# A two-layer mixer encoder on one core: how the first quarter's modulation is summed, and in which order the start is issued

## The chip, the core and the metric

The kernel runs on one core of one Trainium2 chip. The metric is the time of one execution in device microseconds (us), lower is better; three runs of the kernel before gave 649.83, 650.28 and 650.92, median 650.28.

## The reference, cut to what matters

`x` is (1, 512, 1024), `c` is (1, 1024), and there are two layers. Cut to the parts around the change:

```
cs = jax.nn.silu(c)
for l in range(DEPTH):
    mod = cs @ w_ada[l] + b_ada[l]
    shift, scale, gate = jnp.split(mod, 3, axis=-1)
    h = rms_norm(x, norm_g[l]) * (1.0 + scale[:, None]) + shift[:, None]
    proj = h @ w_in[l]                       # 1024 x 3712
    ...                                      # A attention, B windowed attention, C retention
    oc = retention_bidir(qc, kc, vc.reshape(B, S, H_C, DV_C), ret_decay[l], gn_c[l])
    ...
    y = jnp.concatenate([oa, ob, oc], axis=-1) @ w_out[l]
    x = x + gate[:, None] * y
```

`retention_bidir` begins with `log_g = log_sigmoid(ret_decay)`, 8 numbers a layer.

## The kernel before, in words

The 512 tokens are four tiles t of 128, the 1024 features four **quarters** q of 256 (numbered 0 to 3; the first is also called quarter 1 in the change's title). A product of float32 accuracy is made of three float32r products: each operand is split into a part `hi`, rounded by ScalarE (ACT), and a rest `lo` that VectorE (DVE) subtracts.

The start of layer 0 runs quarter by quarter, and a quarter needs the following.

- **Modulation.** `class Start` sums `w_ada` over the 1024 numbers of `cs`, which lie as 8 rows r of 128 partitions. `load` brings two rows into a `raw` buffer (there are five), `row` adds one row to `ada_acc` (the first row of a quarter by ACT, the others by DVE, one 128x512 instruction each), and `close` sums `ada_acc` over the partitions with four matmuls of one moving column (`over_rows`, into `ada_ps`). DVE then makes `mod` of it, the shift and scale. `open` puts the bias in `ada_ps` first. In quarter 0 the rows in `PE_ROWS` go to TensorE (PE) instead.
- **x, turned.** `norm_x` makes `xn` (ACT sums squares, GpSimd takes the root, ACT and DVE scale), `turn_x` transposes four 128x128 blocks on PE into one PSUM tile `xps`, and ACT copies them to `xT`.
- **h.** `turn` makes `hT` (ACT, from `xT` and `mod`), the same unrounded as `h` (DVE), and `hL = h - hT` (DVE).
- **The weights.** `Wide` loads 768 columns of `w_in` as `whi` and `wlo` (three buffers each) and splits them: `stq` and `stB` are the rounded parts (ACT), `stk` and `stC` the rests (DVE).
- **The products.** One group is one (q, t): six products of 512 columns into `acc` and six of 256 into `scw`, at lines 338 (hi by hi), 339 (lo by hi) and 340 (hi by lo). Sixteen groups make the first chunk; `issue(lo, hi)` emits them.

The names in profile rows follow: `stq`/`stk` are the weights of quarters 0 and 2, `stB`/`stC` those of 1 and 3, and `whi`/`wlo` as operands of PE belong to the chunk that comes after (a plan of groups with loads and splits tied to group numbers, the same before and after).

The order of the first steps is the string `START`: each letter is a step (`x` loads and normalizes a token tile, `a` loads and adds two rows of quarter 0, `r` of quarter 1, `t` turns two token tiles of one quarter, `h` makes `h` for two token tiles, `w`/`v` load and `s` splits weights, `f` closes quarter 0). After it comes a loop over quarters 1 to 3, in which `close`, the next loads, `split`, `turn` and `issue` follow each other. A scheduler then sets each engine's own order; all engines work their lists in order, and all DMAs are issued by SyncE (SP). `setup` makes small tables, the last of them the decays: a chain of some 25 instructions of 16 elements on DVE.

Of the kernel before, what the change touches and what calls it, by code (L numbers as in the profile page):

```python
# [19 lines left out]
P = 128  # L20
# [33 lines left out]
PE_ROWS = (0, 2, 4, 5, 6, 7), (), (), ()  # L54


START = "xxbiaaataxfxwrthsttthttrvrrt"
# [18 lines left out]
_SMALL = {"lambda_q1": 32, "lambda_k1": 32, "lambda_q2": 32, "lambda_k2": 32, "ret_decay": 8,  # L76
# [12 lines left out]
N_PARAM = _params()  # L89
N_ONCE = _PARAM["qn_a"][0]  # L90
# [43 lines left out]
def encoder(ctx, tc, x, c, norm_g, w_ada, b_ada, w_in, w_out, params, consts, out):  # L134
# [91 lines left out]
    def setup_loads():  # L226
        once.append(ep.tile([P, N_ONCE], F32, name="once", tag="e"))
        dma(once[0], params[:, :N_ONCE])
        dma(prm, params[:, N_ONCE:])
        dma(cst[:, P:], consts[:, P:N_KEEP])  # L230

    def setup():
# [22 lines left out]


        NL = L * 8
        dec = pr("ret_decay").rearrange("p l n -> p (l n)")
# [231 lines left out]
    class Start:  # L490
# [11 lines left out]
        def open(self):  # L502
            q = self.q
            self.ps = ps = pv_p.tile([P, 2, 2], F32, name="ada_ps", tag="pv")
            self.a = self.line = None

            T.matmul(ps, bias[:2 * KD, 0], ident[:2 * KD].rearrange("p (a j k) -> p a j k", j=2, k=KD)[:, 0, :, 2 * q:2 * q + 2], start=True, stop=False)
# [18 lines left out]
        def close(self):  # L526
            q, ps = self.q, self.ps
            if self.a is not None:
                self.over_rows(self.a, ones[:, 0:1], self.line is None)
            if self.line is not None:  # L530
                z = one.tile([P, 512], F32, name="lsb", tag="s9")
                act(z[0:1], self.line[0:1])
                self.over_rows(z[0:1], ones[0:1, 0:1], True)
            m = self.m = one.tile([P, 2, 2], F32, name=f"mod0{q}")
            stt(m[:, 1], ps[:, 1], 1.0, ngt[:, 2 * q:2 * q + 2], OP.add, OP.mult)
            V.tensor_copy(m[:, 0], ps[:, 0])

        def turn(self, ts):
# [4 lines left out]
            for k in range(2):  # L543
# [4 lines left out]
                V.tensor_scalar(h[:, :n], x_, scale, shift, OP.mult, OP.add)  # L548
# [658 lines left out]
    def turn_x(t, q):  # L1207
        ps = acc_p.tile([P, 2, 2, P], F32, name="xps", tag="acc")
# [17 lines left out]
    def start_end():  # L1226
# [15 lines left out]
    for q in range(1, 4):  # L1242
# [56 lines left out]
```

## Time and profile before

| | us |
|---|---|
| median of three runs | 650.28 (649.83 to 650.92) |
| the profiled execution | 653.0 |
| its span in the profile | 651.2 |
| PE busy | 625.5 (96%) |
| DVE busy | 496.8 (76%) |
| ACT busy | 340.2 (52%) |
| GpSimd busy | 164.4 (25%) |

The profile shows one execution. Times in its rows count from the start of the span, and the profiled execution took 1.8 us more than its span. PE's own busy share counts matmuls that overlap, so that 96% says that PE nearly always has something in hand, not that it runs at its peak.

### The profile page before, as it was taken

What the parts mean: (1) busy time and instruction counts of PE and PEld (TensorE: products, weight loads), DVE (VectorE), ACT (ScalarE), POOL (GpSimd) and SP (SyncE); (2) the same over time, 40 slices, a digit from 0 to 9 for tenths busy, and PEclk for the clock granted to TensorE, in tenths of its full rate; (3) what the DMA queues carried; (4) which work ended last, traced back from release to release, by engine and by line L of the source; (5) the groups of instructions that cost most, each with busy time, mean ns of one, the idle gap of its engine ahead of it and who ended that gap; (6) DMA issues with size and microseconds to landing.
All of it is one profiled execution on the core that took longest, in us unless ns stands there. A gap on an engine that the chain in (4) does not pass through costs nothing.

```text
span 651.2 us, 10473 instructions
## 1 busy us (share of the span) xinstructions
PE 625.5 (96%) x3487; PEld 514.2 (79%) x3487; DVE 496.8 (76%) x1212; ACT 340.2 (52%) x750; POOL 164.4 (25%) x183
## 2 busy tenths in 40 slices
PE   6999999999999996999999999999999999899997
PEld 1878888987888873677779998997788787677786
DVE  1889776789978986997869374778997996677543
ACT  4744362666746665564434244455756567656410
POOL 1105462514360510200411041632323340010000
PEclk9799999999999998999999999999999999999999
DMA  9987123426565557476643322235555453603211
GB/s 315 334 290 207 40 82 88 133 91 152 147 177 167 125 172 175 141 254 224 185 169 96 90 72 67 77 101 154 142 171 137 142 142 103 163 32 139 89 64 65
DMA packets 87133, 93.03 MB, mean 143 GB/s; under 512 B 7044, under 2 KB 68132, under 8 KB 87080
## 3 DMA queue, kind: packets, MB, share of 16 engines
q1 hardware_dynamic: 87080, 92.37, 47.8%
q8 instruction: 28, 0.46, 0.3%
q14 instruction: 25, 0.20, 0.1%
HBM read 72.42 MB, written 4.19 MB: 118 GB/s over the span
## 4 chain that ended last, share of the span: by engine, by line
PE 77%; DVE 11%; issue 5%; POOL 3%; DMA 2%; ACT 2%; SPq 0%; POOLq 0%; ACTq 0%; DVEq 0%
PE acc L338 15%; PE acc L340 15%; PE acc L339 15%; PE tr L555 8%; PE pv L701 5%; PE sc L724 2%; PE acc L334 2%; PE acc L335 1%; PE acc L336 1%; DVE ada_acc L158 1%; PE sc L785 1%; DVE wlo L307 1%; PE sc L786 1%; PE line L519 1%; PE co L954 1%
## 5 line engine op out<-in xcount | busy, mean ns | idle before, releaser
L338 PE MATMUL acc<-whi,hT 128*128 128x384 f32 (+1 forms) x424 | 155.1, 366 | 0.0
L339 PE MATMUL acc<-wlo,hT 128*128 128x384 f32 (+1 forms) x424 | 152.3, 359 | 0.0
L340 PE MATMUL acc<-whi,hL 128*128 128x384 f32 (+1 forms) x424 | 152.0, 358 | 0.0
L307 DVE TENSOR_TENSOR wlo<-raw,whi 128x384 fp32r<-128x384 f32 (+1 forms) x130 | 81.8, 658 | 27.0 <-ACT whi L155 26.7
L198 POOL TENSOR_TENSOR qkss<-qkss,nhalf 128x4 f32<-128x4 f32 (+1 forms) x40 | 52.6, 1316 | 128.3 <-DVE qkss L570 125.7
L338 PEld LDWEIGHTS acc<-whi,hT 128*128 128x128 f32 x424 | 79.9, 188 | 6.1
L340 PEld LDWEIGHTS acc<-whi,hL 128*128 128x128 f32 x424 | 79.8, 188 | 6.2
L339 PEld LDWEIGHTS acc<-wlo,hT 128*128 128x128 f32 x424 | 79.9, 188 | 5.5
L155 ACT ACTIVATE whi<-raw 128x768 fp32r<-128x768 f32 (+2 forms) x67 | 59.6, 890 | 36.8 <-PE acc L340 34.0
L158 DVE SCALAR_TENSOR_TENSOR ada_acc<-raw,cs,ada_acc 128x512 f32<-128x512 f32 x86 | 64.4, 750 | 7.1 <-DMA raw<-in_w_ada_dram 5.9
L155 ACT ACTIVATE e<-sc,mx 128x512 f32<-128x512 f32 x64 | 43.9, 688 | 35.8 <-DVE mx L726 17.2
L726 DVE TENSOR_REDUCE mx<-sc 128x1 f32<-128x512 f32 x64 | 43.5, 685 | 9.6 <-PE sc L724 9.1
L155 ACT ACTIVATE sb<-sb,mx 128x512 f32<-128x512 f32 x48 | 34.4, 717 | 20.5 <-DVE mx L790 20.2
L701 PE MATMUL pv<-pt,v 128*64 128x256 f32 x320 | 40.1, 394 | 0.6 <-DVE pt L691 0.5
L155 ACT ACTIVATE pt<-tr 128x512 f32<-128x512 f32 x40 | 23.8, 596 | 24.2 <-PE tr L555 24.1
L790 DVE CUSTOM_DVE_ANT_0 sb<-sc,cst 128x512 f32<-128x512 f32 x48 | 32.1, 684 | 5.4 <-PE sc L786 3.5
L555 PE MATMUL tr<-cst,sb 128*128 128x128 f32 x192 | 30.5, 282 | 5.3 <-DVE nat L158 2.2
L701 PEld LDWEIGHTS pv<-pt,v 128*64 128x64 f32 x320 | 21.7, 140 | 16.6 <-DVE pt L691 5.3
L555 PEld LDWEIGHTS tr<-cst,sb 128*128 128x128 f32 x192 | 22.1, 142 | 15.8 <-ACT pt L155 7.3
L691 DVE COPY pt<-tr 128x512 f32<-128x512 f32 x40 | 27.4, 684 | 8.4 <-PE tr L555 8.4
L622 POOL TENSOR_TENSOR qkn<-qkraw,qkss 128x256 f32<-128x256 f32 x40 | 30.4, 760 | 5.8 <-DVE qkraw L618 2.0
L724 PE MATMUL sc<-stk,stq 96*128 96x512 f32 x64 | 27.3, 434 | 0.9 <-ACT e L155 0.9
(293 smaller groups left out, 1368.9 us busy)
## 6 DMA issues: line engine op xcount, KB each, us to landing
raw<-in_w_ada_dram SPq DMA_DIRECT2D x64, 256.0 KB, 4.8
raw<-in_w_in_dram SPq DMA_DIRECT2D x48, 192.0 KB, 2.6
raw<-in_w_in_dram SPq DMA_DIRECT2D x24, 384.0 KB, 3.9
raw<-in_w_in_dram SPq DMA_DIRECT2D x32, 256.0 KB, 3.6
raw<-in_w_ada_dram SPq DMA_DIRECT2D x16, 512.0 KB, 5.4
raw<-in_w_out_dram SPq DMA_DIRECT2D x32, 256.0 KB, 2.8
x<-in_x_dram SPq DMA_DIRECT2D x8, 512.0 KB, 3.5
stB<-nat SPq DMA_DIRECT2D x32, 128.0 KB, 2.3
```

Source lines behind the costliest of these rows:

```text
L155: A.activation(o, i, f, **kw)
L158: V.scalar_tensor_tensor(o, a, s, b, op0, op1)
L198: G.tensor_tensor(o, i, nhalf[:, :n], OP.pow)
L307: V.tensor_tensor(l2[:, z], r2[:, z], h2[:, z].bitcast(F32), OP.subtract)
L338: T.matmul(ps, ah, hi[i], start=s_, stop=False)
L339: T.matmul(ps, ah, lo[i], start=False, stop=False)
L340: T.matmul(ps, al, hi[i], start=False, stop=e_)
L555: T.transpose(ps[:, i, :], b, ident)
L701: T.matmul(self.pv[h * 64:h * 64 + 64, i * 256:i * 256 + 256], self.u.v[:, k, h * 64:h * 64 + 64], self.pt[h][:, k], start=k == 0, stop=k ...
L724: T.matmul(ps, self.u.stq[0:96, m, tok_(qt)], self.u.stk[0:96, m], start=True, stop=True)
L726: V.tensor_reduce(mx, ps, AX.X, OP.max, negate=True)
L790: V.tensor_tensor_reduce(sb, ps, cst[:, m0:m0 + S], 1.0, 3e38, OP.add, OP.min, mx)
```

## The change

Of quarter 0's rows, four instead of six go to PE, and each is used as a stationary operand with one moving column of `cs`, straight into `ada_ps`; the other four are added on ACT and DVE. The transposed blocks use the one PSUM buffer of tag `tr` instead of the four of tag `acc`. `START` is another order: `d` starts the decays' chain with a load of its own, the weights `w` and their split `s` come before the last two tiles of `x`, and `g` issues the groups of token tiles 0 and 1, then 2 and 3, of quarter 0 before the remaining transpositions. In quarters 2 and 3, and in half of quarter 1, `h` is made by ACT instead of DVE. In the loop each quarter's groups are issued in its own pass, and the small tables' loads (`setup_loads`) come before the next quarter's rows.

```
-PE_ROWS = (0, 2, 4, 5, 6, 7), (), (), ()
-START = "xxbiaaataxfxwrthsttthttrvrrt"
+PE_ROWS = (0, 2, 4, 6), (), (), ()
+START = "xxbidaaatawsfhgxxrthgttrttrvrtt"
...
+    def decays():
         NL = L * 8
-        dec = pr("ret_decay").rearrange("p l n -> p (l n)")
+        dec = one.tile([P, NL], F32, name="dec")
+        dma(dec, params[:, :N_DEC])
...
             if r in PE_ROWS[self.q]:
-                if self.line is None:
-                    self.line = acc_p.tile([P, 512], F32, name="line", tag="acc")
-                T.matmul(self.line[0:1], v, w, start=r == PE_ROWS[self.q][0], stop=r == PE_ROWS[self.q][-1])
+                self.over_rows(w, v)
...
             else:
-                stt(self.a, w, v, self.a, OP.mult, OP.add)
+                i = V.scalar_tensor_tensor(self.a, w, v, self.a, OP.mult, OP.add)
+                if self.q > 1 and r == 2:
+                    tc.keep_in_program_order(i)
...
-            if self.line is not None:
-                z = one.tile([P, 512], F32, name="lsb", tag="s9")
-                act(z[0:1], self.line[0:1])
-                self.over_rows(z[0:1], ones[0:1, 0:1], True)
...
-                V.tensor_scalar(h[:, :n], x_, scale, shift, OP.mult, OP.add)
+                if q > 1 or q and k:
+                    act(h[:, :n], x_, AF.Identity, bias=shift, scale=scale)
+                else:
+                    V.tensor_scalar(h[:, :n], x_, scale, shift, OP.mult, OP.add)
...
-        ps = acc_p.tile([P, 2, 2, P], F32, name="xps", tag="acc")
+        ps = tr_p.tile([P, 2, 2, P], F32, name="xps", tag="tr")
...
+        if q == 2:
+            setup_loads()
         if q < 3:
             mod = Start(q + 1)
             mod.load()
             first[q + 1].load()
-        if q == 2:
-            setup_loads()
         first[q].split()
         cur.turn(range(NT))
-        issue(4 * q - 4, 4 * q)
-    issue(12, 16)
+        issue(4 * q, 4 * q + 4)
```

Three places show how the engines' own orders move. Numbers behind a name tell buffers apart: `mod00` to `mod03` belong to quarters 0 to 3.

**DVE, around the end of quarter 0's sum.** Before (`ada_acc_164` is that sum, `xn` the normalized x, `ngt` the transposed norm gains):

```order
L1229 COPY ngt_113<-gps_198 128x8
L1205 TENSOR_SCALAR xn_146<-x1_94,rstd_147 128x512
L1205 TENSOR_SCALAR xn_136<-x0_93,rstd_137 128x512
L158 SCALAR_TENSOR_TENSOR ada_acc_164<-raw_166,cs_101,ada_acc_164 128x512
L570 TENSOR_SCALAR rstd_191<-rstd_191 128x1
L1205 TENSOR_SCALAR xn_189<-x2_95,rstd_191 128x512
L158 SCALAR_TENSOR_TENSOR mod00_211<-ada_ps_157,ngt_113 128x2
L536 COPY mod00_211<-ada_ps_157 128x2
```

Now (`ada_acc_198` is the sum, `lu`, `lz` and `lg` belong to the decays; twenty-three more of their instructions stand ahead of this piece, with two more additions among them):

```order
L274 TENSOR_SCALAR lu_159<-lu_159 128x16
L525 SCALAR_TENSOR_TENSOR ada_acc_198<-raw_223,cs_101,ada_acc_198 128x512
L275 TENSOR_TENSOR lu_159<-lu_159,lz_160 128x16
L159 SCALAR_TENSOR_TENSOR lg_117<-lu_159,lg_117 128x16
L159 SCALAR_TENSOR_TENSOR mod00_248<-ada_ps_189,ngt_113 128x2
L535 COPY mod00_248<-ada_ps_189 128x2
L550 TENSOR_SCALAR h_252<-xT0_126,mod00_248 128x256
L550 TENSOR_SCALAR h_256<-xT1_127,mod00_248 128x256
L385 TENSOR_TENSOR stk_236<-whi_231,stq_235 128x2x384
L551 TENSOR_TENSOR hL_119<-h_252,hT_118 128x256
L385 TENSOR_TENSOR stk_236<-wlo_232,stq_235 128x2x384
L551 TENSOR_TENSOR hL_119<-h_256,hT_118 128x256
```

The decays' chain and two more additions now stand ahead of `mod00`, and the splits of the weights directly behind it; x's third tile comes after them.

**PE, where quarter 2's sum over partitions stands.** Before (`ada_ps_415` is quarter 2's; the products around it are quarter 1's last group):

```order
L338 MATMUL acc_402<-stB_349,hT_118 128x512
L512 MATMUL ada_ps_415<-ones_104,ada_acc_417 128x1 x4
L339 MATMUL acc_402<-stC_350,hT_118 128x512
L340 MATMUL acc_402<-stB_349,hL_119 128x512
L338 MATMUL acc_402<-stB_349,hT_118 128x512
L339 MATMUL acc_402<-stC_350,hT_118 128x512
L340 MATMUL acc_402<-stB_349,hL_119 128x512
L338 MATMUL scw_124<-stB_349,hT_118 128x256
```

Now (`ada_ps_503` is quarter 2's, `ada_ps_611` quarter 3's):

```order
L341 MATMUL scw_124<-stB_438,hT_118 128x256
L342 MATMUL scw_124<-stC_439,hT_118 128x256
L343 MATMUL scw_124<-stB_438,hL_119 128x256
L515 MATMUL ada_ps_503<-ones_104,ada_acc_505 128x1 x4
L510 MATMUL ada_ps_611<-cst_103,bias_112 128x4
L341 MATMUL acc_259<-stq_541,hT_118 128x512
L342 MATMUL acc_259<-stk_542,hT_118 128x512
```

Before, eleven products of quarter 1 follow quarter 2's sum; now it stands behind quarter 1's last product and directly ahead of quarter 2's first. Quarter 3's sum moved in the same way, behind quarter 2's last product.

**ACT, between quarters 2 and 3.** Before (`ada_acc_520` is quarter 3's sum, its first row is ACT's):

```order
L155 ACTIVATE stq_453<-wlo_346 128x2x384
L155 ACTIVATE ada_acc_520<-raw_433,cs_101 128x512
L155 ACTIVATE hT_118<-xT4_130,mod02_430 128x512
L155 ACTIVATE hT_118<-xT5_131,mod02_430 128x512
L155 ACTIVATE stB_536<-whi_445 128x2x384
```

Now (`ada_acc_613` is quarter 3's):

```order
L156 ACTIVATE stq_541<-wlo_435 128x2x384
L156 ACTIVATE lsum_661<-lsum_661 128x4
L156 ACTIVATE hT_118<-xT4_130,mod02_518 128x512
L156 ACTIVATE h_548<-xT4_130,mod02_518 128x512
L156 ACTIVATE hT_118<-xT5_131,mod02_518 128x512
L156 ACTIVATE h_552<-xT5_131,mod02_518 128x512
L156 ACTIVATE ada_acc_613<-raw_525,cs_101 128x512
```

Quarter 3's first row stood ahead of the instructions that wait for `mod02`, and now stands behind four of them.

## Rows read from the trace of the kernel before

**Rows 1.** The page: the span, and the busy time of each engine.

```profile
span 651.2 us, 10473 instructions
PE 625.5 (96%) x3487; PEld 514.2 (79%) x3487; DVE 496.8 (76%) x1212; ACT 340.2 (52%) x750; POOL 164.4 (25%) x183
```

**Rows 2.** Busy time of each engine in stretches: stretch, its length, busy us (instructions) of PE, PE's weight loads, DVE, ACT and POOL, then the granted TensorE clock, the DMA engines' busy share and GB/s.

```profile
58.00:102.00 44.00, 44.00 (x256) 38.21 (x255) 35.80 (x122) 20.62 (x50) 21.99 (x20) 1.00 0.27 78
102.00:104.00 2.00, 0.85 (x7) 0.56 (x7) 1.30 (x5) 0.47 (x1) 0.00 (x0) 1.00 0.14 25
```

**Rows 3.** PE's instructions in order of time: the first main product of quarters 0, 1, 2 and 3, and of the next chunk (start us, duration us, engine, line, operation).

```profile
24.91 0.63 PE L338 MATMUL acc<-stq,hT 128*128 128x512 f32 x1
...
34.91 0.50 PE L338 MATMUL acc<-stB,hT 128*128 128x512 f32 x1
...
44.71 0.51 PE L338 MATMUL acc<-stq,hT 128*128 128x512 f32 x1
...
55.99 0.39 PE L338 MATMUL acc<-stB,hT 128*128 128x512 f32 x1
...
64.39 0.39 PE L338 MATMUL acc<-whi,hT 128*128 128x512 f32 x1
```

**Rows 4.** The chain that ended last, in order of time: start us, length us, engine, tile, line.

```profile
25.53 0.43 PE acc L339
...
26.55 0.24 PE acc L339
...
46.60 0.75 DVE ada_acc L158
...
48.18 0.70 DVE hL L549
...
48.92 0.50 PE acc L340
...
96.24 0.88 PE kv L921 x8
```

**Rows 5.** PE in order of time: the first bias and gain products, quarter 0's line sums and its partition sum, the last eight transpositions of x, and a partition sum of later; x counts passes.

```profile
6.52 0.56 PE L507 MATMUL ada_ps<-cst,bias 16*128 16x4 f32 x2 [4.17 <-DMA cst<-in_consts_dram]
6.94 0.25 PE L1228 MATMUL gps<-cst,bias 8*128 8x8 f32 x1
7.12 6.22 PE L519 MATMUL line<-raw,cs 128*1 128x512 f32 x8
...
15.67 1.05 PE L512 MATMUL ada_ps<-ones,ada_acc 128*128 128x1 f32 x8
...
22.93 1.97 PE L1211 MATMUL xps<-cst,xn 128*128 128x128 f32 x8
...
41.54 0.95 PE L512 MATMUL ada_ps<-ones,ada_acc 128*128 128x1 f32 x8
```

**Rows 6.** DVE and POOL in order of time: the end of quarter 0's `mod`, a root on POOL, six additions in a row, and the first and last of the decays' chain from its ninth instruction on (18 of them).

```profile
17.81 0.15 DVE L536 COPY mod<-ada_ps 128x2 f32<-128x2 f32 x1
...
18.88 0.54 POOL L198 TENSOR_TENSOR rstd<-rstd,nhalf 128x1 f32<-128x1 f32 x1 [2.41 <-DVE rstd L570]
...
42.67 4.68 DVE L158 SCALAR_TENSOR_TENSOR ada_acc<-raw,cs,ada_acc 128x512 f32<-128x512 f32 x6
...
61.21 0.17 DVE L270 TENSOR_TENSOR lu<-lu,lq 128x16 f32<-128x16 f32 x1
...
64.77 0.17 DVE L158 SCALAR_TENSOR_TENSOR lg<-lu,lg 128x16 f32<-128x16 f32 x1
```

**Rows 7.** Groups of instructions by line and shape, from 0 to 65 us: busy us, mean ns of one, then idle us before them.

```profile
L382 DVE TENSOR_TENSOR stk<-whi,stq 128x768 fp32r<-128x768 f32 x2 | 1.9, 952 | 0.0
L549 DVE TENSOR_TENSOR hL<-h,hT 128x256 fp32r<-128x256 f32 x4 | 1.5, 418 | 0.0
...
L155 ACT ACTIVATE xT<-xps 128x256 f32<-128x256 f32 x16 | 4.9, 424 | 4.9 <-PE xps L1211 4.9
L155 ACT ACTIVATE hT<-xT,mod 128x512 fp32r<-128x512 f32 x6 | 4.6, 810 | 15.7 <-DVE mod L536 15.7
L155 ACT ACTIVATE junk<-x 128x1024 f32<-128x1024 f32 x4 | 4.2, 1052 | 2.3 <-DMA x<-in_x_dram 2.3
L155 ACT ACTIVATE ada_acc<-raw,cs 128x512 f32<-128x512 f32 x4 | 3.0, 739 | 0.0
L155 ACT ACTIVATE hT<-xT,mod 128x256 fp32r<-128x256 f32 x4 | 2.2, 620 | 0.0
L155 ACT ACTIVATE xn<-x,rstd 128x512 f32<-128x512 f32 x3 | 2.1, 716 | 0.4 <-POOL rstd L198 0.2
L155 ACT ACTIVATE stq<-wlo 128x768 fp32r<-128x768 f32 x2 | 1.7, 837 | 0.0
```

**Rows 8.** Stretches around the changes of the granted clock, and around the wait of 46.9 to 48.9 us; columns as in rows 2.

```profile
19.00:19.50 0.50, 0.40 (x4) 0.16 (x2) 0.04 (x1) 0.50 (x2) 0.42 (x1) 0.77 1.10 363
19.50:20.00 0.50, 0.00 (x1) 0.01 (x1) 0.50 (x2) 0.50 (x2) 0.00 (x0) 0.50 1.05 369
26.00:26.50 0.50, 0.50 (x3) 0.39 (x3) 0.50 (x2) 0.50 (x4) 0.00 (x0) 0.91 1.09 346
46.00:48.00 2.00, 1.31 (x7) 0.77 (x5) 1.97 (x4) 0.46 (x1) 0.07 (x1) 1.00 1.07 352
48.00:50.00 2.00, 1.08 (x5) 0.89 (x6) 2.00 (x4) 0.00 (x0) 0.62 (x1) 1.00 1.22 294
```

More of the change, by code (lines that the diff above doesn't have):

```diff
@@ L73 @@
 N_KEEP = _CONST["ropec"][0]
-_SMALL = {"lambda_q1": 32, "lambda_k1": 32, "lambda_q2": 32, "lambda_k2": 32, "ret_decay": 8,
+_SMALL = {"ret_decay": 8, "lambda_q1": 32, "lambda_k1": 32, "lambda_q2": 32, "lambda_k2": 32,
           "qn_a": 32, "kn_a": 32, "qn_b": 64, "kn_b": 64}
@@ L89 @@
 N_PARAM = _params()
+N_DEC = _PARAM["lambda_q1"][0]
 N_ONCE = _PARAM["qn_a"][0]
@@ L218, in pr @@
         o, n = _PARAM[name]
-        z, o = (prm, o - N_ONCE) if o >= N_ONCE else (once[0], o)
+        z, o = (prm, o - N_ONCE) if o >= N_ONCE else (once[0], o - N_DEC)
         return z[:, o:o + L * n].rearrange("p (l n) -> p l n", l=L)
@@ L226, in setup_loads @@
     def setup_loads():
-        once.append(ep.tile([P, N_ONCE], F32, name="once", tag="e"))
-        dma(once[0], params[:, :N_ONCE])
+        once.append(ep.tile([P, N_ONCE - N_DEC], F32, name="once", tag="e"))
+        dma(once[0], params[:, N_DEC:N_ONCE])
         dma(prm, params[:, N_ONCE:])
@@ L504, in open @@
             self.ps = ps = pv_p.tile([P, 2, 2], F32, name="ada_ps", tag="pv")
-            self.a = self.line = None
+            self.a = None
             T.matmul(ps, bias[:2 * KD, 0], ident[:2 * KD].rearrange("p (a j k) -> p a j k", j=2, k=KD)[:, 0, :, 2 * q:2 * q + 2], start=True, stop=False)
@@ L523, in row @@
             else:
-                stt(self.a, w, v, self.a, OP.mult, OP.add)
+                i = V.scalar_tensor_tensor(self.a, w, v, self.a, OP.mult, OP.add)
+                if self.q > 1 and r == 2:
+                    tc.keep_in_program_order(i)
         def close(self):
             q, ps = self.q, self.ps
-            if self.a is not None:
-                self.over_rows(self.a, ones[:, 0:1], self.line is None)
-            if self.line is not None:
-                z = one.tile([P, 512], F32, name="lsb", tag="s9")
-                act(z[0:1], self.line[0:1])
-                self.over_rows(z[0:1], ones[0:1, 0:1], True)
+            self.over_rows(self.a, ones[:, 0:1], True)
             m = self.m = one.tile([P, 2, 2], F32, name=f"mod0{q}")
@@ L1234, in encoder @@
              "r": [(lambda r: start_rows(mod1, r), r) for r in range(0, KD, 2)], "v": [(lambda _: first[1].load(), 0)],
-             "i": [(lambda _: dma(cst[:, :P], consts[:, :P]), 0)], "b": [(lambda _: bias_loads(), 0)], "w": [(lambda _: first[0].load(), 0)], "s": [(lambda _: first[0].split(), 0)],
+             "i": [(lambda _: dma(cst[:, :P], consts[:, :P]), 0)], "b": [(lambda _: bias_loads(), 0)], "d": [(lambda _: decays(), 0)], "w": [(lambda _: first[0].load(), 0)], "s": [(lambda _: first[0].split(), 0)],
              "f": [(lambda _: start_end(), 0)], "t": [(lambda z: turn_x(*z), (t, q)) for q in range(4) for t in (0, 2)],
-             "h": [(mod.turn, (0, 1)), (mod.turn, (2, 3))]}
+             "h": [(mod.turn, (0, 1)), (mod.turn, (2, 3))], "g": [(lambda g: issue(g, g + 2), 0), (lambda g: issue(g, g + 2), 2)]}
     for z in START:
```

## The prediction, made before the changed kernel ran

> **What bounds the kernel now.** I read the page first: PE has work in hand for 96% of the span, DVE for 76% [rows 1]. The stretches come next: from 58 to 102 us PE is busy for 44.0 of 44.0 us, and its next loss is in 102 to 104 [rows 2]. That loss is no grace for a late start: in the chain it follows from PE's own `kv` products at 96.24 [rows 4], and would come later with them. So whatever the start of layer 0 gains or loses up to about 56 us is handed on in full, and the change touches nothing behind it in PE's order. The quantity to forecast is therefore the moment at which quarter 3's products begin, 55.99 us; the next chunk follows 8.4 us later without a pause [rows 3].
>
> Inside the start the quarters' products begin at 24.91, 34.91, 44.71 and 55.99 [rows 3]. Two steps are of 10 us, the last is of 11.3: there the chain of waits leaves PE. DVE makes six additions of quarter 3 before quarter 2's `h` and `hL`, and PE goes on at 48.92 [rows 4]. The two windows around it show PE busy 1.31 and 1.08 of 2 us each, so about 1.6 us are lost [rows 8]. This is the only larger wait after 25 us that a better order could remove.
>
> **Prices.** A 512-column product takes 0.43 us at the low clock and 0.24 at the full one [rows 4]; a quarter at full clock 8.4 us [rows 3]. A partition sum (8 passes) takes 0.95 at full clock; at the low one a pass takes 0.21, from the three passes between 6.52 and 7.12 [rows 5]. An addition on DVE takes 0.78, being in a row of six that each need the last [rows 6]. An instruction of the decays takes 0.21: eighteen from 61.21 to 64.98 [rows 6].
>
> The Trainium skill (TensorE: Matmul & The Clock Gate, section LDWEIGHTS) gives a load of P stationary columns as P/1.2 ns, an estimated 0.107 us for 128, with no clock in it. Our row of 0.21 at the low clock [rows 5] disagrees; by the page the partition sum would take half, `mod` would be ready an estimated 1.0 us sooner, and the forecast would be 657.5. I take the row.
>
> **Quarter 0's sum: nothing gained.** The twelve passes of the line, its ACT copy and eight passes of partition sum go; 32 passes of one column come, of 0.21 each, or 1.7 us a row, 0.95 if the clock were full. From 7.2 on PE has them done at about 15.2, with four transposed blocks between the first two (0.24 each [rows 5]). But DVE is later: its additions stand among the decays. The chain's long part starts at about 9.5, an estimate, behind `xn` and ACT's exponential; 21 instructions of 0.21 (4.4) and two additions (1.2, as they overlap what is ahead) later the last addition starts at 15.1 and ends at 15.8. Eight passes of 0.21 and `mod` lead to 17.9; now `mod` is there at 17.96 [rows 6]. At 0.12 a pass it would be 16.9, so the term is 0, with -1.0 as its lower bound.
>
> **First products early, but slow and then paid for.** ACT goes `hT` (0.6), `stq` (0.8), so PE begins at 19.4 instead of 24.91. DVE's two `h`, split (0.95), `hL`, split bring the second operand at 20.9 [rows 7]. Two groups are 24 products, 4.2 us at full clock, twice that at half; with the clock up at about 24.5 they end at 26.1. Now 24.91 finds all 32 transpositions done; then only four will be. The other 28 are due with one PSUM buffer: each four wait until ACT has copied the last four (0.7), where four buffers now let PE run on.
>
> **Quarter 1 starts 3.5 late.** x's last tiles land behind the weights, and ACT takes them after `hT`: squares (1.05 and 0.2 of readout), root (0.55 [rows 6]), `xn` on ACT (0.7), squares, root [rows 7], then two `xn` on DVE: from 19.9 on with the hand-overs, done at 25.7. Only now may DVE add quarter 1: seven additions (5.4), two `h`, two `hL` (0.4 each), two splits (0.95) and a wait of 0.9 for `xT`, which comes after the two groups: 35.2 us. The partition sum ends at 36.2, `mod`, behind another addition, at 36.6, a copy of `xT` and `hT` (0.8) on ACT follow: PE starts quarter 1 at 38.4, against 34.91. Groups 2 and 3 do not fill the time: they are done by 32.4, and the transpositions left need about 2 us.
>
> **Quarter 2 loses 1.3 more.** Its products of quarter 1 and the last four transpositions take 8.9 us, to 47.3. Then the order puts the partition sum behind the last product, with nothing behind it to cover `mod` and `hT`: 0.95 + 0.25 + 0.8 + the bias pass, so 49.5 against 44.71: +4.8. DVE waits too, from about 46 on, because `mod` stands in its list before quarter 3's additions.
>
> **Quarter 3 loses 2.4 more.** The wait of 1.6 us in quarter 2 is gone: `h` comes from ACT. But ACT now does four instructions of 0.75 (48.6 to 51.6) before quarter 3's first row (to 52.3), and DVE's seven additions (5.4) have two `wlo` of 512 columns (0.65 each, in proportion to the splits) and two splits (0.87 each, net of overlap) between them: 60.8. PE has been through with quarter 2 since 57.8. Partition sum (0.95), `mod` (0.4), `hT` (0.8) and hand-overs make 63.2. Against 55.99 that is **+7.2**.
>
> **The clock.** From 57.8 to 63.2 PE has no product but eight one-column passes. In the trace the granted clock fell from 1.00 to 0.50 near 19.3 after such a stretch: sixteen one-column passes from 15.67 and transpositions [rows 5, 8]; it was back near 26.1. After the loss of 46.9 to 48.9 it stayed at 1.00 [rows 8]. A stretch of 5.4 us is nearer to the first. A fall costs half of the product time that runs slow, between 0 and 3 us; most of the low stretch lies in the wait itself, so I take +1.0. A second fall can come between 32 and 38 (bound +1.5).
>
> **What costs nothing.** `dec`'s load is 8 KB behind 1 MB of x. Moving the decays and the tables out of 57 to 65 us frees DVE where PE is busy all the time, so it gains nothing there [rows 2]. The loads of the tables ahead of quarter 3's rows take 2.5 us at the DMA's 350 GB/s [rows 8]. Seven of those rows are already used by 47.4 now [rows 4], so 2.5 us later they are still there before ACT asks at 51.6.
>
> **The sum.** 653.0 for the profiled execution + 7.2 + 1.0 = 661.2. The median is 2.7 below that execution, so 650.28 + 8.2 = **658.5**.
>
> **Rivals.** (1) The start holds its old pace: additions of quarter 1 get done by 31.7, quarter 1 begins at 34.9, and only the uncovered sums of quarters 2 and 3 remain: 7.2 - 3.5 = +3.7 without a fall, 654.0. For it: the first products are early. Against: DVE's list, where nothing of quarter 1 may pass `xn`. (2) The clock falls twice, or for longer: +7.2 + 3 + 1.5 = +11.7, 662.0. [...] (3) Faster: PE fills 19.4 to 24.9 with two groups (-4.2) and the wait at 46.9 is gone (-1.6), nothing else being late: 644.5. It decides at quarter 3's last addition: if that ends before 55 us, while quarter 2's products still run, the order pays. My chain has it at 60.8, so 5.8 us of DVE and ACT time would have to be wrong. (4) No change: early groups and late sums cancel, 650.3.
>
> **How the numbers follow.** Forecast 0.75, rival 1 0.10, rival 2 0.06, rival 3 0.05, rival 4 0.04. Rivals 1 and 2 are slower too: slower by over 0.2% (1.3 us, about what a measurement of this kernel tells from none) 0.91, same 0.04, faster 0.05. The range runs from rival 1 to rival 2, 654.0 to 662.0: inside the forecast lie -1.0 for the passes, -1.0 for the clock, +2 and +1.5.
>
> **What would show it.** In the new profile: `mod` of quarter 0 near 17.9; first product near 19.4; DVE idle and waiting on PE near 46 to 48; the last addition of quarter 3 near 61, and PE idle for some 3 us before its partition sum; quarters at 38.4, 49.5 and 63; PEclk 0.5 somewhere in 58 to 67. I am wrong if quarter 3's products begin before 57, which needs its additions to start before quarter 2's `h`; or if a later stretch than 102 us shrinks, which nothing in the order speaks for.

## The result, and the profile of the changed kernel

The changed kernel is slower: median 661.41 us (659.61 to 663.26, four runs) against 650.6, ratio 1.0146, 95% interval 1.0112 to 1.0179. The ratios in this document are estimates with their intervals and not quotients of two medians (that quotient is 1.0166 here). Timed again on another chip beside other kernels it had 659.66 against 651.18, ratio 1.0144 (1.0124 to 1.0164). The profiled execution took 661.1 us, 8.1 more than that of the kernel before. The forecast was 658.5, in a range of 654.0 to 662.0: the median lies 0.6 us inside its upper end, and one of the four runs beyond it.

The page's first lines, to be read against [rows 1]: TensorE (PE) is busy for 2.7 us more and DVE for 2.9 us less, while the span is 8.1 us longer.

```profile
span 659.3 us, 10492 instructions
PE 628.2 (95%) x3499; PEld 522.0 (79%) x3499; DVE 493.9 (75%) x1209; ACT 343.9 (52%) x754; POOL 160.2 (24%) x183
```

PE in order of time: one of quarter 0's rows (eight one-column passes), the first products of quarters 0 to 3 and of the next chunk, two products following each other, and the partition sums of quarters 1, 2 and 3. In brackets stands the idle time before a row and what ended it.

```profile
7.22 1.84 PE L515 MATMUL ada_ps<-cs,raw 128*128 128x1 f32 x8
...
19.69 0.80 PE L341 MATMUL acc<-stq,hT 128*128 128x512 f32 x1 [0.78 <-ACT stq L156]
...
22.20 0.63 PE L341 MATMUL acc<-stq,hT 128*128 128x512 f32 x1
22.62 0.63 PE L342 MATMUL acc<-stk,hT 128*128 128x512 f32 x1
...
34.86 1.05 PE L515 MATMUL ada_ps<-ones,ada_acc 128*128 128x1 f32 x8 [0.34 <-DVE ada_acc L525]
...
37.86 0.59 PE L341 MATMUL acc<-stB,hT 128*128 128x512 f32 x1
...
48.38 0.95 PE L515 MATMUL ada_ps<-ones,ada_acc 128*128 128x1 f32 x8
...
50.55 0.50 PE L341 MATMUL acc<-stq,hT 128*128 128x512 f32 x1 [0.47 <-ACT hT L156]
...
61.57 1.05 PE L515 MATMUL ada_ps<-ones,ada_acc 128*128 128x1 f32 x8 [0.80 <-DVE ada_acc L525]
63.78 0.50 PE L341 MATMUL acc<-stB,hT 128*128 128x512 f32 x1 [1.17 <-ACT hT L156]
...
72.32 0.39 PE L341 MATMUL acc<-whi,hT 128*128 128x512 f32 x1
```

Against [rows 3] quarter 0 begins 5.2 us sooner, quarter 1 2.95 later, quarter 2 5.84 later, quarter 3 7.79 later, the next chunk 7.93 later. Nearly all of the 8.1 us is there before the next chunk begins. (Against a second trace of the kernel before, e11 below, the next chunk is 7.0 later.)

DVE and ACT show why. First DVE: quarter 0's last addition, `xn` of x's last tile, quarter 1's last addition (the first of this pair), the last small table, quarter 2's `mod`, quarter 3's first and last addition on DVE.

```profile
15.28 0.74 DVE L525 SCALAR_TENSOR_TENSOR ada_acc<-raw,cs,ada_acc 128x512 f32<-128x512 f32 x1
...
24.78 0.88 DVE L1207 TENSOR_SCALAR xn<-x,rstd 128x512 f32<-128x512 f32 x2 [0.66 <-POOL rstd L199]
...
34.06 1.41 DVE L525 SCALAR_TENSOR_TENSOR ada_acc<-raw,cs,ada_acc 128x512 f32<-128x512 f32 x2
...
44.92 0.32 DVE L159 SCALAR_TENSOR_TENSOR nlam<-lsum 128x1 f32<-128x1 f32 x2
49.37 0.16 DVE L159 SCALAR_TENSOR_TENSOR mod<-ada_ps,ngt 128x2 f32<-128x2 f32 x1 [4.13 <-PE ada_ps L515]
...
53.27 0.75 DVE L525 SCALAR_TENSOR_TENSOR ada_acc<-raw,cs,ada_acc 128x512 f32<-128x512 f32 x1
...
60.77 0.74 DVE L525 SCALAR_TENSOR_TENSOR ada_acc<-raw,cs,ada_acc 128x512 f32<-128x512 f32 x1
```

Then ACT: quarter 0's first `hT` and the squares of x's third tile; the first and last of quarter 2's four `hT` and `h`, and behind them quarter 3's first row.

```profile
18.30 0.60 ACT L156 ACTIVATE hT<-xT,mod 128x256 fp32r<-128x256 f32 x1 [3.21 <-DVE mod L535]
...
20.04 1.04 ACT L156 ACTIVATE junk<-x 128x1024 f32<-128x1024 f32 x1
...
49.69 0.81 ACT L156 ACTIVATE hT<-xT,mod 128x512 fp32r<-128x512 f32 x1 [4.83 <-DVE gcol L235]
...
51.82 0.80 ACT L156 ACTIVATE h<-xT,mod 128x512 f32<-128x512 f32 x1
52.53 0.71 ACT L156 ACTIVATE ada_acc<-raw,cs 128x512 f32<-128x512 f32 x1
```

DVE stands idle for 4.13 us until quarter 2's sum, which PE makes only at 48.38, behind quarter 1's last product. ACT waits for the same `mod` (the row names `gcol`, which follows it on DVE), and quarter 3's first row stands behind its `hT` and `h`. Only from 53.27 does DVE add quarter 3, and PE waits for its end at 61.5.

Stretches (columns as in rows 2; the third figure from the end is the granted clock):

```profile
20.00:22.00 2.00, 1.95 (x5) 1.25 (x5) 1.52 (x4) 1.17 (x3) 0.40 (x1) 1.00 1.09 356
38.00:40.00 2.00, 2.00 (x9) 1.81 (x10) 1.97 (x4) 1.93 (x5) 0.55 (x2) 0.53 1.15 315
40.00:42.00 2.00, 2.00 (x9) 1.67 (x9) 1.97 (x4) 2.00 (x4) 0.38 (x1) 0.61 1.01 373
52.00:54.00 2.00, 2.00 (x7) 1.54 (x6) 1.35 (x3) 2.00 (x4) 0.14 (x1) 0.50 0.03 8
60.00:62.00 2.00, 1.20 (x11) 1.00 (x9) 2.00 (x3) 1.06 (x1) 0.00 (x0) 1.00 1.12 311
```

The clock was at its low level in two stretches, about 38 to 41.5 and 52 to 55, but not after PE's wait at 61.

### The profile page after: what moved, and what is told of

Its sections match the earlier page's. It is cut to its first block, busy times and chain, and to the rows that moved or that the text cites. A ratio compares the mean times of both kernels' runs of the same rounds, so it can differ in the third digit from the quotient of the medians.

```text
span 659.3 us, 10492 instructions
## 1 busy us (share of the span) xinstructions
PE 628.2 (95%) x3499; PEld 522.0 (79%) x3499; DVE 493.9 (75%) x1209; ACT 343.9 (52%) x754; POOL 160.2 (24%) x183
## 4 chain that ended last, share of the span: by engine, by line
PE 76%; DVE 11%; issue 5%; POOL 3%; ACT 3%; DMA 1%; SPq 1%; DVEq 0%; POOLq 0%; ACTq 0%
PE acc L341 15%; PE acc L343 15%; PE acc L342 15%; PE tr L557 8%; PE pv L703 5%; PE sc L726 2%; PE acc L339 1%; PE acc L337 1%; DVE ada_acc L525 1%; PE acc L338 1%; PE sc L787 1%; PE ada_ps L515 1%; DVE wlo L310 1%; PE sc L788 1%; PE co L956 1%
## 5 line engine op out<-in xcount | busy, mean ns | idle before, releaser
L156 ACT ACTIVATE e<-sc,mx 128x512 f32<-128x512 f32 x64 | 44.0, 689 | 35.4 <-DVE mx L728 16.8
L159 DVE SCALAR_TENSOR_TENSOR ada_acc<-raw,cs,ada_acc 128x512 f32<-128x512 f32 x64 | 48.0, 750 | 5.0 <-DMA raw<-in_w_ada_dram 4.7
L703 PEld LDWEIGHTS pv<-pt,v 128*64 128x64 f32 x320 | 21.8, 140 | 16.7 <-DVE pt L693 5.3
```

The source lines that it names most:

```text
L156: A.activation(o, i, f, **kw)
L159: V.scalar_tensor_tensor(o, a, s, b, op0, op1)
L703: T.matmul(self.pv[h * 64:h * 64 + 64, i * 256:i * 256 + 256], self.u.v[:, k, h * 64:h * 64 + 64], self.pt[h][:, k], start=k == 0, stop=k ...
```

## The experiments

Start of each quarter's products and of the next chunk in every trace (us, one execution each), and the ratio of timed runs to the kernel before on the same chip:

| kernel | ratio (95% interval) | q1 | q2 | q3 | next chunk |
|---|---|---|---|---|---|
| before, two traces (the second is e11) | 1 | 34.91, 35.81 | 44.71, 45.62 | 55.99, 56.90 | 64.39, 65.30 |
| changed | 1.0146 (1.0112 to 1.0179) | 37.86 | 50.55 | 63.78 | 72.32 |
| changed again (e5) | 1.0144 (1.0124 to 1.0164) | 38.14 | 49.32 | 62.55 | 72.58 |
| e1 issue back | 1.0040 (1.0023 to 1.0057) | 37.61 | 49.21 | 58.64 | 67.01 |
| e2 h on DVE | 1.0104 (1.0081 to 1.0128) | 37.89 | 50.57 | 63.11 | 71.63 |
| e3 decays last | 1.0145 (1.0117 to 1.0173) | 39.50 | 51.77 | 65.14 | 75.98 |
| e4 zero products | 1.0124 (1.0101 to 1.0147) | 38.87 | 50.07 | 63.31 | 73.33 |
| e6 e1 with the old start | 1.0044 (1.0024 to 1.0063) | 39.46 | 49.26 | 58.69 | 67.08 |
| e7 rows alone | 1.0042 (1.0026 to 1.0058) | 35.75 | 45.54 | 56.83 | 65.23 |
| e8 old order | 1.0032 (1.0016 to 1.0048) | 35.57 | 45.44 | 56.37 | 66.42 |
| e9 e7, squares first | 1.0030 (1.0009 to 1.0051) | 35.27 | 45.07 | 56.34 | 64.73 |
| e10 e6, four buffers | 1.0017 (1.0001 to 1.0032) | 36.67 | 46.48 | 56.87 | 65.36 |
| e12 e10, x's chain first | **0.9959 (0.9940 to 0.9979)** | 33.59 | 43.36 | 53.41 | 61.91 |

**e1: the issue put back.**

```
-        issue(4 * q, 4 * q + 4)
+        if q > 1:
+            issue(4 * q - 4, 4 * q)
+    issue(12, 16)
```

> The changed kernel, with only the loop's issue put back: a quarter's groups are issued one pass later again, so that other products can cover the next quarter's partition sum. Theory A (most of the loss is the partition sums of quarters 2 and 3 that nothing covers, and DVE's additions held behind them): in the trace of the changed kernel quarter 1's products end at 48.4 and quarter 2's begin at 50.55; covered, quarter 2 begins at about 48.5 and quarter 3 8.4 us later, at 57, instead of 63.78. That is -5 to -7 us, so 654.5 to 656.5, and what is left against the kernel before is the late quarter 1 (37.86 against 34.91). Rival B (the one PSUM buffer for the transposed blocks and the late x hold everything, and the clock falls that follow): nothing of that is touched, so 660 to 662. Rival C (TensorE's low stretches at 38.0 and 51.9 are the loss, 1.7 us each): the first stays, the second may go, -1.7, so 659.7.

Ratio 1.0040 where the changed kernel has 1.0146: 1.06%, some 7 us, come back with three lines. PE in order of time:

```profile
43.72 0.95 PE L515 MATMUL ada_ps<-ones,ada_acc 128*128 128x1 f32 x8
...
49.21 0.50 PE L341 MATMUL acc<-stq,hT 128*128 128x512 f32 x1
...
55.30 0.95 PE L515 MATMUL ada_ps<-ones,ada_acc 128*128 128x1 f32 x8
...
58.64 0.39 PE L341 MATMUL acc<-stB,hT 128*128 128x512 f32 x1
```

Both sums now lie inside the quarter ahead, with products behind them, and neither quarter's first product shows a wait. Theory A holds, B and C fall: the median is 654.55, and the low stretch in quarter 1 is still there (about 37 to 40.5).

**e2: h made by DVE again.**

```
-                if q > 1 or q and k:
-                    act(h[:, :n], x_, AF.Identity, bias=shift, scale=scale)
-                else:
-                    V.tensor_scalar(h[:, :n], x_, scale, shift, OP.mult, OP.add)
+                V.tensor_scalar(h[:, :n], x_, scale, shift, OP.mult, OP.add)
```

> The changed kernel, with only h of quarters 1 to 3 made by DVE again. Theory A: in the changed kernel ACT makes hT, h, hT, h (49.69 to 52.5) before quarter 3's first row, and DVE waits meanwhile (idle 1.06 and 0.72 us before the two hL). With h on DVE two of ACT's four 0.71 us go, the first row comes 1.4 us sooner, DVE's additions of quarter 3 start about 1.4 sooner and quarter 3's products with them: -1 to -2.5 us, 659 to 660.4. Rival D (DVE is the bound of the start, so that the move to ACT helps and only the rest of the change costs): two h of 0.45 us a quarter come back to DVE's list, +1 to +2 us, 662.4 to 663.4.

ACT in order of time, behind quarter 2's `mod`:

```profile
49.71 1.52 ACT L156 ACTIVATE hT<-xT,mod 128x512 fp32r<-128x512 f32 x2 [3.82 <-DVE mod L535]
51.13 0.71 ACT L156 ACTIVATE ada_acc<-raw,cs 128x512 f32<-128x512 f32 x1
```

Quarter 3's first row starts at 51.13 instead of 52.53, 1.4 sooner as reckoned, and DVE's last addition of quarter 3 ends at 58.6 instead of 61.5. Quarter 3's products begin only 0.67 sooner, because PE itself is not through with quarter 2 before 60.6; 63.11 also lies between the two traces of the changed kernel. The ratio is 1.0104 where that kernel has 1.0146 and 1.0144, with intervals that just overlap. D falls (its 662.4 to 663.4 against 659.1). Theory A has the place right; that `h` on ACT costs time in this order is likely, but not clear of noise.

**e3: the decays last.** The `d` of the start's string moves to its end (`"xxbiaaatawsfhgxxrthgttrttrvrttd"`).

> The changed kernel, with only the decays' chain moved from ahead of quarter 0's rows to the end of the start's string. Theory A: quarter 0's last addition then ends not at 16.0 but about 1 us sooner, mod and the first products 0.5 to 1 us sooner, but quarter 1 still waits for x's last tiles on DVE (xn done at 25.66) and its seven additions, so quarter 1 begins where it did: 0 to -0.7 us, 660.7 to 661.4. Rival E (the chain ahead is what makes the start late): its 25 instructions of 0.21 us, less what overlaps, are handed on, -2.5 us or more, 659 or less.

No change in time, as A says, but not by A's working: quarter 0's first product is at 19.71 as before, since PE now goes from its row passes straight into the partition sum at 16.12, and quarter 1 begins 1.6 us later. PE, around quarter 1's sum:

```profile
35.98 0.66 PE L1213 MATMUL xps<-cst,xn 128*128 128x128 f32 x4 [0.75 <-ACT xT L156]
36.48 0.95 PE L515 MATMUL ada_ps<-ones,ada_acc 128*128 128x1 f32 x8
```

In the changed kernel this sum (34.86) has two blocks of transpositions between quarter 0's last products and itself; here it has three, and the third waits for ACT's copies of the second. DVE does not hold it, as its last addition ends at 35.5 and the chain follows from 35.45 on. The other 0.7 us is there from 27.11 on, where the transpositions behind the first groups begin (26.39 in the changed kernel). So E falls, and the edit also changed the order on PE. (The next chunk at 75.98 is that of the slowest of the five executions, with a low stretch from about 64 to 70.)

**e4 and e5: the clock.**

```
+        pieces[0].zeros = y, w.rearrange("p a n -> p (a n)")
...
+    def fill(n):
+        y, w = first[0].zeros
+        for _ in range(n):
+            T.matmul(w, y[:, :P], y, start=False, stop=False)
...
         mod.close()
+        fill(3)
```

> The changed kernel with three more products of 512 columns of zeros per quarter (added to an accumulator that they do not change), issued at the closing of quarters 1, 2 and 3, where TensorE has only transpositions, one-column passes and waits. They ask whether the low clock of 38.0 to 41.5 and 51.9 to 55.2 costs time. Theory A (the first low stretch is handed on, 1.7 us, because quarter 2 begins when quarter 1's products end; the second is hidden, because quarter 3 waits for DVE's last addition at 61.5 while TensorE is through at 60.8): if the clock stays up, quarter 2 begins at 48.9 instead of 50.55, and the time is -1.7, 659.7; if it falls all the same, 661.4. Rival C (both stretches are the loss): -3.4, 658. Rival F (the products are in the way, since TensorE is the bound): +0.7 to +2.2 us, 662 to 663.6.

> The changed kernel as it is, timed beside the three below on the same chip. The first time gave a ratio of 1.0146 to the kernel before, so 1.011 to 1.018 again; by theory A its trace shows quarter 3's products beginning between 63 and 64.5 us and DVE idle for some 4 us until quarter 2's partition sum.

Stretches of e4:

```profile
38.00:40.00 2.00, 1.79 (x12) 1.34 (x12) 2.00 (x4) 1.96 (x5) 0.53 (x1) 1.00 1.09 339
40.00:42.00 2.00, 2.00 (x14) 1.78 (x12) 1.96 (x4) 2.00 (x5) 0.53 (x1) 1.00 1.10 346
64.00:66.00 2.00, 2.00 (x8) 1.61 (x7) 1.40 (x3) 1.38 (x2) 0.41 (x1) 0.50 0.86 240
```

and of the unaltered changed kernel, in a second trace:

```profile
38.00:40.00 2.00, 1.95 (x12) 1.59 (x12) 1.96 (x4) 1.96 (x5) 1.01 (x2) 1.00 1.18 306
58.00:60.00 2.00, 0.00 (x0) 0.00 (x0) 2.00 (x4) 0.78 (x1) 0.00 (x0) 1.00 1.06 290
62.00:64.00 2.00, 1.45 (x5) 1.26 (x6) 2.00 (x4) 2.00 (x4) 0.00 (x0) 0.68 0.78 213
64.00:66.00 2.00, 2.00 (x7) 1.52 (x6) 0.75 (x2) 0.62 (x1) 0.41 (x1) 0.50 0.95 276
```

In e4 the clock stayed up from 38 to 42 and quarter 1 took 11.20 us to quarter 2, not 12.69. Quarter 1 itself came 1.0 later, but the zero products are not the reason: the lateness is there at 27.39, where the transpositions behind the first groups begin (26.39 in the changed kernel), and the first zero product runs at 33.96. So quarter 2 began at 50.07 and not at A's 48.9; F falls with 660.41 against its 662 to 663.6. And e5 had no low stretch at 38 to 42 either, without any zero products, and took 11.18. So what one trace shows of the clock belongs to that execution, and e4 does not show that the products kept it up; its ratio, 1.0124, has an interval that overlaps those of the changed kernel. (e5's ratio is as expected; its quarter 3, at 62.55, is half a microsecond ahead of the range, and DVE's wait is 2.61 us, not some 4.) What the two traces of the changed kernel do show is the price: with the low stretch in quarter 1, quarter 2 begins 1.2 later (50.55 against 49.32); with it in quarter 3 (e5), quarter 3 takes 10.03 us to the next chunk and not 8.54. The next chunk begins at 72.32 and 72.58, nearly the same. Rival C, both stretches added up as the loss, falls: e5 has neither, and its quarter 3 still begins 5.6 us later than in the second trace of the kernel before.

**e6: the old start on top of e1.** `START = "xxbidaaataxfxwrthsttthttrvrrt"`, and the loop's issue of the kernel before.

> The changed kernel with the order of the start and the loop's issue of the kernel before; the decays' chain stays early, and the stationary rows, the one PSUM buffer for transposed blocks, h on ACT and the early tables stay. The run with the issue alone put back had quarter 1 at 37.61, quarter 3 at 58.64 and a ratio of 1.004. Theory A (what is left there is the start's order: x's last tiles behind the weights, DVE's additions behind them): quarter 1 begins near 35 again, quarter 3 near 56, ratio 0.998 to 1.001. Rival H (what is left is the one PSUM buffer, at which TensorE waits 0.75 us for each block's copies): the start's order makes no difference, quarter 1 still begins at 37 to 39, ratio 1.002 to 1.006.

Ratio 1.0044, quarter 1 at 39.46: theory A is wrong here, and H's ratio holds (its quarter 1 is half a microsecond past the range). The start's order alone was not what kept quarter 1 late. ACT shows what the two orders have in common:

```profile
18.91 0.60 ACT L156 ACTIVATE hT<-xT,mod 128x256 fp32r<-128x256 f32 x1 [7.59 <-DVE mod L535]
19.42 1.04 ACT L156 ACTIVATE junk<-x 128x1024 f32<-128x1024 f32 x1
```

As in the changed kernel (18.30 and 20.04), the first `hT` stands ahead of the third tile's squares and waits for `mod`. With the old order x's last `xn` is done at 24.9, only 0.8 sooner.

**e10: four PSUM buffers on top of e6.** One line: `tr_p ... tag="tr"` becomes `acc_p ... tag="acc"` for `xps`. (With the new start's string this was not tried, since there the four `acc` buffers are held by the groups already begun.)

> The run with the old start and the issue put back (ratio 1.0044; quarter 1 at 39.46, quarter 3 at 58.69), with the transposed blocks in the four PSUM buffers again; the decays stay early. In that run TensorE's five blocks of transpositions from 26.30 on come every 1.35 to 1.4 us, each behind ACT's two copies, with quarter 0's products between them. Theory M (the one buffer spaces the transpositions and holds the products of quarter 0): quarter 1 at 37 to 38, quarter 3 at 57 to 57.7, ratio 1.001 to 1.003. Rival N (what holds that run is the early decays and ACT's squares behind hT, both unchanged here): quarter 1 at 39 or later, ratio 1.004 or more.

Quarter 1 at 36.67, 2.8 sooner, ratio 1.0017: M holds in the trace, if not to the decimal (the blocks of e6 come 1.35 to 2.5 us apart, not all within 1.4); the two ratios' intervals overlap. Of the 2.8 us, 0.5 is there from PE's first bias product on (7.19 in e6, 6.65 here). Another part comes by a way that M does not name: the one buffer also takes the gains' transposition `gps`, and in e6 DVE waits 0.63 us for it ahead of quarter 0's additions (0.62 in the changed kernel), which it does not here. Quarter 1 is still 0.9 to 1.8 behind the kernel before.

**e7: the rows alone, put into the kernel before.**

```
-PE_ROWS = (0, 2, 4, 5, 6, 7), (), (), ()
+PE_ROWS = (0, 2, 4, 6), (), (), ()
...
-                if self.line is None:
-                    self.line = acc_p.tile([P, 512], F32, name="line", tag="acc")
-                T.matmul(self.line[0:1], v, w, start=r == PE_ROWS[self.q][0], stop=r == PE_ROWS[self.q][-1])
+                self.over_rows(w, v)
```

> The kernel before with one part of the change: four of quarter 0's rows as stationary operands, the other four added by ACT and DVE; nothing else. In the run with the decays last, TensorE went without a wait from its last one-column pass to the partition sum at 16.12, and mod followed at about 18. Theory A: mod is not there sooner than the 17.96 of the kernel before, and the time is the same, ratio 0.998 to 1.002. Rival I (what the title says: the copy and the second sum are gone, so mod comes 1 us sooner and all behind it): ratio 0.998 or less. Rival J (the six rows as 512-column products kept TensorE's clock up from 12.5 to 19.3; without them the first products of quarter 0, at 24.9, run at the low level for longer, as they did from 19.7 to 24.4 in the changed kernel): +1 to +2 us, ratio 1.0015 to 1.003.

ACT in order of time:

```profile
16.76 0.60 ACT L155 ACTIVATE hT<-xT,mod 128x256 fp32r<-128x256 f32 x1 [4.57 <-DVE mod L534]
17.26 1.04 ACT L155 ACTIVATE junk<-x 128x1024 f32<-128x1024 f32 x1
```

`mod` is there at 16.66, 1.3 us sooner than in the kernel before [rows 6], so A's first half is wrong and I's is right. Yet the first 512-column product came at 26.24, 1.3 later than in [rows 3] (0.4 later than in the second trace of the kernel before). ACT waited 4.57 us for `mod` with `hT`, and x's third tile, whose squares the kernel before takes at 14.51, stood behind it. Ratio 1.0042: none of the three had that reason, and J's falls in PE's rows:

```profile
26.24 0.39 PE L338 MATMUL acc<-stq,hT 128*128 128x512 f32 x1
26.47 0.40 PE L339 MATMUL acc<-stk,hT 128*128 128x512 f32 x1
```

Quarter 0's products follow each other by 0.23 us from the first on, where the kernel before begins with 0.43 [rows 4]. The trace's next chunk (65.23) is no later than in the second trace of the kernel before (65.30). So this trace does not show where the 0.42% lies; that ACT's wait is its cause is argued here, and tested on another kernel in e12.

**e8: the whole change in the old order.** Old start with `d` at its end, old issue, four buffers.

> The changed kernel with the start's order, the loop's issue and the four PSUM buffers of the kernel before, the decays' chain at the start's end. What stays of the change: stationary rows, h by ACT in quarters 2 and 3 (and half of quarter 1), the tables' loads before quarter 3's rows, and the decays before the first chunk's end. Theory A: the order and the issue carried the whole loss, so nothing is lost against the kernel before, and the wait of 1.6 us between quarter 2's products may go, since h no longer stands behind DVE's six additions: ratio 0.996 to 1.000. Rival K (h on ACT or the early tables lose by themselves, by delaying the first row of quarter 3 or its loads): ratio 1.002 to 1.005.

Ratio 1.0032. The number is K's, but its cause is not: quarter 3 begins no later than with the rows alone (56.37 against 56.83), so `h` on ACT and the early tables cost nothing up to there that a trace could show (its next chunk is late by a low stretch of the clock from about 58 to 61). Theory A, that nothing would be lost, fails; this kernel has the rows too, and ACT's first `hT` waits 4.58 us for `mod` as in e7. Next to e10, from which it differs only by the decays' place, quarter 1 begins 1.1 us sooner, and the ratios' intervals overlap.

**e9: squares first, on e7.**

```
+    def first_h(ts):
+        with tc.issue_after(squares[2].ins):
+            mod.turn(ts)
```

> The run with the rows alone (stationary rows put into the kernel before, nothing else), with one more edit: ACT's first hT is queued behind the squares of x's third tile. In the rows-alone run mod came at 16.5 instead of 17.8, but ACT stood idle for 4.57 us until mod, with hT ahead of those squares, which ran at 17.26 instead of 14.51; the third tile's xn came at 19.2 instead of 16.5, the fourth's at 22.6 instead of 20.2, and the first 512-column product at 26.24 instead of 24.91. Theory L (the rows' gain at mod is lost because ACT's order puts hT, which waits for mod, ahead of squares that are ready): the third tile's xn at 16 or before, the fourth's about 21, the first 512-column product at 24.5 to 25, quarter 3's at 55.2 to 55.8 instead of 56.83; ratio to the kernel before 0.998 to 1.002 where rows alone gave 1.0042. Rival J (the clock, not the squares: without the six 512-column products TensorE is at the low level for longer): ratio 1.003 to 1.005 again.

ACT took the squares at 13.85. DVE did not follow:

```profile
16.94 0.74 DVE L546 TENSOR_SCALAR h<-xT,mod 128x256 f32<-128x256 f32 x2
17.59 0.15 DVE L568 TENSOR_SCALAR rstd<-rstd 128x1 f32<-128x1 f32 x1
...
18.39 0.49 DVE L1203 TENSOR_SCALAR xn<-x,rstd 128x512 f32<-128x512 f32 x1 [0.65 <-POOL rstd L198]
```

The next step of x's chain, `rstd`, stands on DVE behind `h`, which waits for `mod` as well. So `xn` came at 18.39, not at 16, and quarter 3 at 56.34, past L's range and only 0.49 sooner than in e7. Ratio 1.0030 against 1.0042: it settles nothing by itself (J's range takes it in, but J's reason fell in e7), and the rows say that the chain has to be freed on both engines.

**e11: the kernel before, a second trace.**

> The kernel before, looked at a second time. Its first profiled execution took 653.0 us, 2.7 above the median of its runs, while that of the changed kernel lay at its median. Theory P (executions of one kernel differ by where TensorE's clock falls: 18 to 26, 250 to 256 and 568 to 574 in the first one): another execution has its low stretches elsewhere or shorter, and quarter 3 begins within 1.5 us of 55.99. Rival Q (the start of layer 0 is the same in every execution): quarter 3 at 55.8 to 56.2 and the low stretches where they were.

653.5 us; everything from quarter 0 on lies 0.9 later than in the first trace, with the low stretch from 20 to 27 instead of 19 to 26. Theory P by half: the stretches are the same ones, shifted. So starts in single traces are good to about 1 us (the two traces of the changed kernel differ by 1.2 at quarters 2 and 3), and smaller differences decide nothing here.

**e12: x's chain first, on e10.**

```
+    def first_h(ts):
+        with tc.issue_after(scaled["A", 2].ins):
+            mod.turn(ts)
...
-        mod.close()
+        with tc.issue_after(scaled["V", 2].ins):
+            mod.close()
```

(`scaled` holds ACT's and DVE's `xn` instructions of each tile.)

> The run with the old start, the issue put back and four PSUM buffers (ratio 1.0017; quarter 1 at 36.67, quarter 3 at 56.87), with one more edit: in quarter 0, DVE's mod is queued behind its xn of x's third tile, and ACT's first hT behind ACT's xn of that tile. There ACT stood idle for 6.96 us until mod (17.71) with hT ahead of the third tile's squares, the xn of the third tile came at 20.19 and that of the fourth at 22.80 to 23.6, and TensorE waited 2.42 us for the first. Squares were taken at 13.85 where only they were queued first. Theory L (the waiting hT and mod ahead of x's ready steps hold the start, whatever else of the change is there): squares 14 to 15.2, third xn at about 16.5, fourth at 19.3 to 20.1, first products about 3 us sooner, quarter 1 at 33.5 to 34.5, quarter 3 at 53.5 to 55 (before 55.99 and 56.90 in two looks), ratio 0.996 to 0.999: faster than both kernels. Rival R (mod and with it h come later, and TensorE, at its low level, takes back what the transpositions gain): quarter 1 at 36 or later, ratio 1.001 to 1.003.

ACT, then DVE, in order of time: the third and the fourth tile's squares; the third tile's `xn`, `mod`, and the fourth's `xn`.

```profile
14.65 1.06 ACT L156 ACTIVATE junk<-x 128x1024 f32<-128x1024 f32 x1 [4.04 <-DMA x<-in_x_dram]
...
17.27 1.04 ACT L156 ACTIVATE junk<-x 128x1024 f32<-128x1024 f32 x1
```

```profile
16.64 0.49 DVE L1207 TENSOR_SCALAR xn<-x,rstd 128x512 f32<-128x512 f32 x1 [0.65 <-POOL rstd L199]
17.20 0.16 DVE L159 SCALAR_TENSOR_TENSOR mod<-ada_ps,ngt 128x2 f32<-128x2 f32 x1
...
19.25 0.88 DVE L1207 TENSOR_SCALAR xn<-x,rstd 128x512 f32<-128x512 f32 x2 [0.66 <-POOL rstd L199]
```

ACT now waits for a transfer, not for `mod`, and `mod` (17.20) loses nothing by standing behind `xn`. The quarters begin 3.1 to 3.5 us sooner than in e10, quarter 3 at 53.41. Ratio 0.9959, interval below 1: median 649.74 against 651.81, by 0.4% faster than the kernel before, and faster than the changed one. L holds. The two orders were changed together, so the share of each is not known.

## Why the prediction was right, point by point

**The steps.** `mod` of quarter 0 was forecast at 17.9, done 18.2; first product 19.4, was 19.69; x's last `xn` done 25.7, was 25.66; DVE done with quarter 1's work 35.2 (the terms given add up to 35.5), the last addition ended at 34.8; quarter 1 at 38.4, was 37.86 and 38.14. The partition sums stand behind the last product, uncovered, as said; DVE is idle from 45.2 to 49.37. Quarter 3's last addition was forecast at 60.8 and ended at 61.5 and 60.3, its products at 63.2, were 63.78 and 62.55. The sum for the profiled execution was 661.2; it took 661.1, the second one 659.7. That the first agrees to 0.1 us is luck, with 1.4 us between the two.

**The passes.** Eight one-column passes at 7.22 take 1.84, at 48.38 0.95: the price of 0.21 at the low level and 0.12 at the full one held (0.23 and 0.12). The Trainium skill (TensorE: Matmul & The Clock Gate, section LDWEIGHTS) has one price for both, an estimated 0.107 for 128 columns; the trace comes near it at the full level only.

**The clock: near in size, in its place in one trace of two.** The term was +1.0 for a fall between 57.8 and 63.2. In the second trace it fell just behind that (0.68 and 0.50 in 62 to 66, after two microseconds without any PE work), and cost 1.5. In the first trace it fell in quarters 1 and 2 instead; the first of these falls cost quarter 2 1.2. The second cost nothing, since DVE was later: PE was through with quarter 2 at 60.8 rather than 57.8, and waited 0.8 us where the forecast had 3.

**The uncovered sums: right, as a net of loss and gain.** I had +1.3 and +2.4 for quarters 2 and 3, net of the 1.6 us that the old wait between `h` and DVE's additions gives back. Put back, the issue brings 5.3 in the traces (72.32 to 67.01), which is 1.3 + 2.4 + 1.6: the loss and the gain were both there. The timed runs give some 7 us (1.0146 to 1.0040), so agreement to the decimal is luck.

**The late quarter 1: right in size, half right in cause.** I laid 3.5 us on x's last tiles, behind the weights in the transfers and behind `hT` on ACT. The trace of the changed kernel shows the chain that I described, down to PE's sum at 34.86, which waits for DVE's last addition. But the weights ahead are not needed for it: with the old start (e6) quarter 1 is as late, and `hT` still stands ahead of x's squares there. Under the old start two other things hold quarter 1: the one PSUM buffer, which I had named but charged only under another heading (2.8 us at quarter 1, e10 against e6), and `hT` and `mod` placed ahead of x's ready steps (3.1 us, e12 against e10). Several limits lay side by side, and taking away one uncovered the next. Neither of the two was undone under the new start, so their shares in the changed kernel itself are not shown. Rival 1, "the start keeps its pace", would have needed more than the old order.

**The rows: "nothing gained" was right here for reasons that do not hold elsewhere.** In the changed kernel `mod` comes at 18.2, as late as before. Moving the decays away is not enough: with the new start and the one buffer it comes at 18.2 again (e3). With the old order, four buffers and the decays early it comes at 17.6 (e10), and with the decays late or where they were at 16.7 to 16.8 (e8, e7), 1.2 to 1.3 us sooner than in [rows 6]. What the order on ACT then makes of that is the wait seen in e7.

**The base.** I took 2.7 off the sum because the first profiled execution lay above the median of three runs. Later medians of the kernel before were 650.6 and, on other chips, 652.1, 651.2, 651.6 and 651.8: the three were probably low, and the offset nearer 1.5. That would be 1.2 of the 2.9 us between 658.5 and 661.41; the rest is within the spread of the runs (659.6 to 663.3, and 659.66 as the second median).

## What to carry to other kernels

A result that becomes ready sooner need not make a program faster: an engine that works its list in order loses time when a consumer that waits stands ahead of work that is ready (e12 against e10: 3 us). Look at each engine's idle time before the consumer, and at what stands behind it. A short reduction that gates the next stage needs products of the stage ahead behind it. Where undoing a part changes nothing, undo two: limits that lie side by side hide each other.

## What the runs showed of the hardware

The granted clock in the rows is 1.00 from 20 to 22 us in the changed kernel, and 1.00 still at 22 to 24, yet products of 512 columns start there every 0.42 us (22.20, 22.62), the pace of the low level, 1.2 GHz [rows 4]. From 24.52 on they start every 0.23 us, with the column at 1.00 as before. So in these traces the column does not show the level before the first recorded fall, and it has to be read from the pace. The pace changes at 24.4 in this trace, and at 25.2 and 26.4 in those of e5 and e4, which are the same program up to there. And the same program has its low stretches in other places in another execution (38 to 41.5 and 52 to 55, or 62 to 66), with nearly the same time for the start as a whole.
